# Adding the gated products to the merged sum by accumulating transfers in place of VectorE additions

## Chip, cores and metric

One Trainium2 chip, one of its cores. The time is the device time of one execution in microseconds, as the median of several executions; the profile is one more execution, recorded by the hardware profiler. Engines: PE is TensorE (PEld its weight loads), DVE is VectorE, ACT is ScalarE, POOL is GpSimd, SP is SyncE, which issues most of the loads.

## What is computed

One layer of a decoder trunk on 256 tokens of width 2048, all in float32. Three token mixers run side by side (a gated recurrence `a`, a windowed attention `b`, a short convolution `c`), each gives a vector of width 1024 per token, and the part that matters here joins them:

```python
y_a = (o_a * jax.nn.silu(a_g)) @ w_proj_hgrn[l]
y_b = (o_b * jax.nn.silu(b_g)) @ w_proj_attn[l]
y_c = (o_c * jax.nn.silu(c_g)) @ w_proj_conv[l]
merged = jax.nn.sigmoid(m_a) * y_a + jax.nn.sigmoid(m_b) * y_b + jax.nn.sigmoid(m_c) * y_c
y = merged @ w_out[l]
x = layer_norm(ALPHA * x + y, ln_g[l], ln_b[l])
```

The gates `m_a`, `m_b`, `m_c` are 2048 columns each of the input projection `x @ w_in`; `merged` and `y` are 256 x 2048.

## The kernel before

Every product of matrices is made from float32 data split into two parts, `hi` (a cast on ACT, line 114) and `lo` (the remainder, a subtraction on DVE, line 115); three matmuls (hi*hi, lo*hi, hi*lo) stand for one. The weights stream from HBM in loads of 1 MB issued by SP into three buffers `raw`. `gemm` (line 165) walks a weight matrix in granules of 1 MB, splits each half granule and issues its matmuls into two PSUM accumulators, one for each half of the 256 tokens (`t` = 0, 1). Between half granules it calls `pump`, which advances a background task by one step.

The merge is the loop over the three branches (lines 742 to 762). For each branch and each half of the 2048 gate columns, `pair_of_groups` (line 667) makes the gate logits of 1024 columns by a scheme with fewer block products, eight or seven of them in turn (matmuls in lines 679 to 681), and leaves them in two tiles `sg`; ACT takes the sigmoid (line 749). Then for each of the two groups of 512 columns (`d` from 0 to 3 in all) `gemm` makes the branch's projection, and DVE multiplies it by the gate. In branch `a` that product is written to `merged[d]`. In branches `b` and `c` it is written back to `sg` (line 757) and added to `merged[d]` by a second instruction (line 758). There are four tiles `merged[d]` of 128 x 2 x 512, each 512 KB, and two tiles `sg`.

In the last half of branch `c`, `turn(merged[d], d)` (line 647) is queued as a background task for every finished tile: it transposes the tile on PE in four groups of 128 x 128 per PSUM bank (`mT`, line 270), casts and subtracts it into the tiles `m` (hi and lo), and for every other pair of blocks makes the sums `msums`. The tasks of d = 0 and 1 run during the projection of d = 2, the task of d = 2 during the projection of d = 3, and the task of d = 3 during the first output product, `gemm(a["w_out"][2], ...)`, which is followed by `pair_of_groups` on `w_out2`, the last quarter and the layer norm. The output product reads `m` of d = 0 first and of d = 3 last (steps k = 12 to 15 of 16).

The order on each engine is not written out by hand: a scheduler places the instructions, with a cost model of its own, and each engine then runs its list in order. A transposition that waits therefore holds up every matmul behind it in PE's list. GpSimd has next to nothing to do between the attention and the layer norm.

Of the kernel before, what the change touches and what calls it, by code (L numbers as in the profile page):

```python
# [13 lines left out]
ALU = mybir.AluOpType  # L14
# [36 lines left out]
def hybrid_kernel(ctx, tc, a, out):  # L51
    nc = tc.nc
# [14 lines left out]
    def t8(shape, name, dt=F32):  # L67
        return w8.tile(shape, dt, tag="w8", name=name)
# [16 lines left out]
    def split_to(dst, src):  # L85

        nc.scalar.copy(out=dst[:, :, 0], in_=src)
        nc.vector.tensor_sub(out=dst[:, :, 1], in0=src, in1=f32(dst[:, :, 0]))
# [77 lines left out]
    def gemm(src, xs, n, major):  # L166


        acc = accumulators()
        per = HALF // n  # L170
        kt = src.shape[0] * 2 * per
        k = 0
        for g in range(src.shape[0]):
            raw = load_granule(src[g])
            for s in range(2):
                hi, lo = split_w(raw[:, s])
                for j in range(per):
                    xk = xs[k // 4][:, k % 4]
                    for b in range(2):
                        c = slice(b * P, b * P + P)  # L180
                        if major == "rows":
                            w = slice(j * n, j * n + n)
                            rows(acc[b][:, :n], xk, hi[:, w], lo[:, w], c, k == 0, k == kt - 1)
                        else:
                            w = slice(j * n + b * P, j * n + b * P + P)
                            columns(acc[b], xk, hi[:, w], lo[:, w], k == 0, k == kt - 1)
                    k += 1
                pump()
        return acc
# [395 lines left out]
    for hf in range(2):  # L585
# [11 lines left out]
        for u in range(2):  # L597
# [3 lines left out]
                             in1=C["gn"][:, hf * NC : hf * NC + NC].rearrange("p (o n) -> p o n", o=1)  # L601
# [51 lines left out]
    def turn(m, d):  # L653
        dst = t8([P, 4, 2, T], "m", F32R)
        ms.append(dst)
        if d % 2 == 0:
            msums.append(t8([P, 2, 4, 2, P], "msums", F32R))
        for i, ps in transpose_pairs([[m[:, t, c * P : c * P + P] for t in range(2)] for c in range(4)], "mT"):
            split_to(dst[:, i : i + 2], ps)
            if PAIRS[2 * d + i // 2]:  # L660
                raw = mgp.tile([P, 2, T], F32, tag="u", name="mraw")
                nc.scalar.copy(out=raw, in_=ps)
                sx = mgp.tile([P, 4, P], F32, tag="one", name="sx")
                block_sums([sx[:, j] for j in range(4)], raw[:, 0, :P], raw[:, 1, :P], raw[:, 0, P:], raw[:, 1, P:])
                split_to(msums[d // 2][:, d % 2], sx)
            yield
# [72 lines left out]
    merged = [mgp.tile([P, 2, NC], F32, tag="merged", name="merged", bufs=4) for _ in range(4)]  # L739
    mix = {"b": yb, "c": yc}  # L740
    for n, (wp, br) in enumerate((("w_proj_hgrn", "a"), ("w_proj_attn", "b"), ("w_proj_conv", "c"))):
        if n:
            for i in range(2):
                outs[br].append(t8([P, 4, 2, T], "o" + br, F32R))
                split_to(outs[br][i], mix[br][:, 4 * i : 4 * i + 4])
        for half in range(2):
            sg = pair_of_groups(a["w_gate"][2 * n + half], xs, sums, n > 0, 2 if n else 1)
            for y in sg:
                nc.scalar.activation(out=y, in_=y, func=AF.Sigmoid)
            if br == "c" and half:  # L750
                tasks.extend(turn(merged[d], d) for d in range(2))
            for j in range(2):
                d = 2 * half + j
                acc = gemm(a[wp][d], outs[br], NC, "rows")
                for t in range(2):
                    if n:
                        nc.vector.tensor_mul(out=sg[j][:, t], in0=acc[t], in1=sg[j][:, t])
                        nc.vector.tensor_add(out=merged[d][:, t], in0=merged[d][:, t], in1=sg[j][:, t])
                    else:
                        nc.vector.tensor_mul(out=merged[d][:, t], in0=acc[t], in1=sg[j][:, t])  # L760
                if br == "c" and half:
                    tasks.append(turn(merged[d], d))

# [167 lines left out]
```

## Time and profile before

| what | value |
|---|---|
| median of 3 runs | 1001.27 us (1000.53 to 1001.45) |
| the profiled execution | 999.9 us, of which the profile's span is 998.0 us |
| PE busy | 984.2 us (99% of the span) |
| DVE busy | 800.5 us (80%) |
| ACT busy | 561.0 us (56%) |
| POOL busy | 31.7 us (3%) |
| DMA | 193.67 MB, mean 194 GB/s over the span |

The table is to be read with the stages in mind. A share of busy time is a mean over the span, and an engine may be idle at one place because it waits there for another. The time of the profiled execution is 1.4 us below the median of the runs; sums are made against it. The span begins with the first instruction and leaves out 1.9 us around it.

### The profile page before, as it was taken

The page shows a single profiled execution, that of the slowest core. Times are in us where ns is not written, and L with a number is a line of the kernel's source. Part 1 is how long each engine was busy: PE and PEld are TensorE (multiplying, and loading weights), DVE is VectorE, ACT ScalarE, POOL GpSimd, SP SyncE. Part 2 cuts the span into 40 slices and gives each one's busy share as a digit, 9 for nine tenths or more (in the row PEclk, how much of TensorE's full clock was granted, in tenths as well). Part 3 has the DMA queues.
Part 4 walks back from the last instruction along what each step waited for, and adds up shares of the span by engine and source line. Part 5 has one row for each costly group of instructions (what it writes and reads, how often), then busy time and mean ns, then how long its engine had stood idle before and what let it go on. Part 6 is the DMA issues. An engine that isn't in the chain of part 4 may idle for free.

```text
span 998.0 us, 13720 instructions
## 1 busy us (share of the span) xinstructions
PE 984.2 (99%) x5430; PEld 828.8 (83%) x5430; DVE 800.5 (80%) x1001; ACT 561.0 (56%) x736; POOL 31.7 (3%) x32
## 2 busy tenths in 40 slices
PE   9999999999999999999999999999999999999995
PEld 6888888888888888888888888888888888888885
DVE  6556689969996666767778898887989889897997
ACT  6454568556576555645655555555555555564551
POOL 1000100020001000000000000000000000000003
PEclk9999999999999999999999999999999999999998
DMA  8755544344455446544555655565655555548542
GB/s 342 253 197 173 206 169 171 146 152 170 169 208 179 181 152 205 175 169 169 196 183 189 227 187 203 207 211 200 214 179 209 210 192 214 185 169 340 208 169 84
DMA packets 30687, 193.67 MB, mean 194 GB/s; under 512 B 3824, under 2 KB 4880, under 8 KB 8352
## 3 DMA queue, kind: packets, MB, share of 16 engines
q1 hardware_dynamic: 28800, 185.90, 52.1%
q10 hardware_dynamic: 1152, 4.72, 1.2%
q0 software_dynamic: 672, 2.20, 0.8%
q8 instruction: 42, 0.69, 0.3%
q14 instruction: 21, 0.17, 0.1%
HBM read 190.68 MB, written 2.12 MB: 193 GB/s over the span
## 4 chain that ended last, share of the span: by engine, by line
PE 92%; DVE 5%; issue 1%; ACT 1%; DMA 1%; POOL 0%; SPq 0%; DVEq 0%; ACTq 0%
PE acc L162 24%; PE acc L161 11%; PE p L679 9%; PE p L680 9%; PE p L681 9%; PE acc L154 8%; PE acc L156 8%; PE acc L155 8%; PE sc L472 1%; DVE lo L115 1%; PE acc L164 1%; PE bg L156 1%; PE bg L154 1%; PE bg L155 1%; PE pvb L514 1%
## 5 line engine op out<-in xcount | busy, mean ns | idle before, releaser
L114 ACT CAST hi<-raw 128x1024 fp32r<-128x1024 f32 (+1 forms) x341 | 343.2, 1013 | 317.4 <-PE p L680 105.0
L115 DVE TENSOR_TENSOR lo<-raw,hi 128x1024 fp32r<-128x1024 f32 (+1 forms) x341 | 398.6, 1179 | 109.4 <-ACT hi L114 107.8
L162 PE MATMUL acc<-xs,hi 128*128 128x512 f32 x1056 | 372.8, 397 | 0.0
L161 PE MATMUL acc<-xs,lo 128*128 128x256 f32 x990 | 279.4, 282 | 0.2 <-DVE lo L115 0.2
L162 PEld LDWEIGHTS acc<-xs,hi 128*128 128x128 f32 x1056 | 197.5, 188 | 44.3 <-issue 1.5
L161 PEld LDWEIGHTS acc<-xs,lo 128*128 128x128 f32 x990 | 186.9, 189 | 4.2 <-issue 1.2
L679 PE MATMUL p<-hi,xs 128*128 128x512 f32 x240 | 93.5, 389 | 0.0
L680 PE MATMUL p<-hi,xs 128*128 128x512 f32 x240 | 93.5, 389 | 0.0
L681 PE MATMUL p<-lo,xs 128*128 128x512 f32 x240 | 93.5, 389 | 0.0
L115 DVE TENSOR_TENSOR lw<-w,hw 128x2048 fp32r<-128x2048 f32 x28 | 64.2, 2293 | 22.2 <-ACT hw L114 20.8
L114 ACT CAST hw<-w 128x2048 fp32r<-128x2048 f32 x28 | 53.5, 1911 | 9.1 <-DVE w L706 8.9
L681 PEld LDWEIGHTS p<-lo,xs 128*128 128x128 f32 x240 | 45.1, 188 | 9.4
L680 PEld LDWEIGHTS p<-hi,xs 128*128 128x128 f32 x240 | 45.1, 188 | 9.3
L679 PEld LDWEIGHTS p<-hi,xs 128*128 128x128 f32 x240 | 45.1, 188 | 9.3
L154 PE MATMUL acc<-hi,xs 128*128 128x512 f32 (+1 forms) x128 | 47.6, 372 | 0.3 <-ACT hi L114 0.3
L199 ACT COPY rest<-acc 128x256 f32<-128x256 f32 x66 | 23.8, 372 | 41.3 <-PE acc L162 40.7
L155 PE MATMUL acc<-hi,xs 128*128 128x512 f32 (+1 forms) x128 | 46.6, 364 | 0.0
L156 PE MATMUL acc<-lo,xs 128*128 128x512 f32 (+1 forms) x128 | 46.1, 364 | 0.0
L704 DVE TENSOR_TENSOR w<-raw 128x1024 f32<-128x1024 f32 x28 | 34.1, 1219 | 0.7 <-DMA raw<-in_w_gate 0.2
L154 PEld LDWEIGHTS acc<-hi,xs 128*128 128x128 f32 x128 | 24.3, 190 | 6.5 <-ACT hi L114 2.2
L680 PE MATMUL p<-hw,sums 128*128 128x512 f32 x72 | 28.0, 390 | 0.0
L679 PE MATMUL p<-hw,sums 128*128 128x512 f32 x72 | 28.0, 389 | 0.0
(269 smaller groups left out, 1505.9 us busy)
## 6 DMA issues: line engine op xcount, KB each, us to landing
raw<-in_w_cols SPq DMA_DIRECT2D x68, 1024.0 KB, 4.8
raw<-in_w_gate SPq DMA_DIRECT2D x48, 1024.0 KB, 4.8
raw<-in_w_out SPq DMA_DIRECT2D x16, 1024.0 KB, 4.8
raw<-in_w_rows SPq DMA_DIRECT2D x8, 1024.0 KB, 4.7
raw<-in_w_proj_hgrn SPq DMA_DIRECT2D x8, 1024.0 KB, 4.8
raw<-in_w_proj_attn SPq DMA_DIRECT2D x8, 1024.0 KB, 4.8
raw<-in_w_proj_conv SPq DMA_DIRECT2D x8, 1024.0 KB, 4.8
raw<-in_w_first SPq DMA_DIRECT2D x6, 1024.0 KB, 7.2
```

The costliest lines, as they stand in the source:

```text
L114: nc.scalar.copy(out=hi, in_=r)
L115: nc.vector.tensor_sub(out=lo, in0=r, in1=f32(hi))
L154: nc.tensor.matmul(out=acc, lhsT=xk[:, 0, ts], rhs=hi, start=first, stop=False)
L155: nc.tensor.matmul(out=acc, lhsT=xk[:, 1, ts], rhs=hi, start=False, stop=False)
L156: nc.tensor.matmul(out=acc, lhsT=xk[:, 0, ts], rhs=lo, start=False, stop=last)
L161: nc.tensor.matmul(out=acc[:, :T], lhsT=lo, rhs=xk[:, 0], start=False, stop=False)
L162: nc.tensor.matmul(out=acc, lhsT=hi, rhs=xk, start=first, stop=last)
L199: nc.scalar.copy(out=rest[p], in_=acc[p, T:])
L679: nc.tensor.matmul(out=ps, lhsT=x[0], rhs=hi, start=begins, stop=False)
L680: nc.tensor.matmul(out=ps, lhsT=x[1], rhs=hi, start=False, stop=False)
L681: nc.tensor.matmul(out=ps, lhsT=x[0], rhs=lo, start=False, stop=last)
L704: nc.vector.tensor_sub(out=w[:, 0:2], in0=raw[:, 0:1].to_broadcast([P, 2, NC]), in1=raw[:, 1::2])
```

## The change

In branches `b` and `c` the 16 additions on DVE (128 x 512 each) are taken out. After both halves `t` of a group have been multiplied, one transfer issued by GpSimd adds the whole tile `sg` (128 x 1024) to `merged[d]` in SBUF, eight transfers of 512 KB in all.

```diff
@@ -755,9 +755,10 @@
                 for t in range(2):
                     if n:
                         nc.vector.tensor_mul(out=sg[j][:, t], in0=acc[t], in1=sg[j][:, t])
-                        nc.vector.tensor_add(out=merged[d][:, t], in0=merged[d][:, t], in1=sg[j][:, t])
                     else:
                         nc.vector.tensor_mul(out=merged[d][:, t], in0=acc[t], in1=sg[j][:, t])
+                if n:
+                    nc.gpsimd.dma_start(out=merged[d], in_=sg[j], accum_op=ALU.add)
                 if br == "c" and half:
                     tasks.append(turn(merged[d], d))
```

Lines below the merge move down by one. The scheduler moves instructions too. On PE the matmuls stand in the same order as before; what moves are the transpositions of d = 2 and d = 3. For d = 2 (during the last projection of branch `c`, whose operands are named `oc`), the difference, where a minus is before and a plus is the change:

```order
-L270 MATMUL mT<-ident,merged 128x128
-L154 MATMUL acc<-hi,oc 128x512
-L155 MATMUL acc<-hi,oc 128x512
-L156 MATMUL acc<-lo,oc 128x512
-L270 MATMUL mT<-ident,merged 128x128 x3
...
+L154 MATMUL acc<-hi,oc 128x512
+L270 MATMUL mT<-ident,merged 128x128 x4
 L155 MATMUL acc<-hi,oc 128x512
 L156 MATMUL acc<-lo,oc 128x512
```

The first transposition of d = 2 stood 12 matmuls behind the last group of transpositions of d = 1; now 22 matmuls stand between them, and its second group of four follows two matmuls behind the first.

For d = 3 (during the first output product, whose operands are named `m`), again on PE:

```order
 L156 MATMUL acc<-lo,m 128x512
-L270 MATMUL mT<-ident,merged 128x128 x4
 L154 MATMUL acc<-hi,m 128x512
...
 L155 MATMUL acc<-hi,m 128x512
+L270 MATMUL mT<-ident,merged 128x128 x4
 L156 MATMUL acc<-lo,m 128x512
 L270 MATMUL mT<-ident,merged 128x128 x4
```

The first group of transpositions of d = 3 stood behind 12 matmuls of the output product; now it stands behind 23, and one matmul ahead of the second group.

On DVE, around the last two groups of branch `c` (d = 2 ahead, d = 3 behind):

```order
 L757 TENSOR_TENSOR sg<-acc,sg 128x512 x2
 L88 TENSOR_TENSOR m<-mT,m 128x2x256
-L758 TENSOR_TENSOR merged<-merged,sg 128x512 x2
+L115 TENSOR_TENSOR lo<-raw,hi 128x1024
...
+L757 TENSOR_TENSOR sg<-acc,sg 128x512
 L555 TENSOR_TENSOR sx<-mraw,sx 128x128
+L757 TENSOR_TENSOR sg<-acc,sg 128x512
...
-L757 TENSOR_TENSOR sg<-acc,sg 128x512 x2
-L758 TENSOR_TENSOR merged<-merged,sg 128x512 x2
```

The additions are gone, a subtraction `lo` of the weights comes one place earlier in their stead, and the products of d = 3 come ahead of a `lo` and the sums `msums` that stood ahead of them. On POOL the eight transfers stand behind the attention's loads of the bias and ahead of the layer norm, with nothing between them.

## Rows read from the trace of the kernel before

**Rows 1.** The page: busy time, share of the span and instructions of each engine.

```profile
PE 984.2 (99%) x5430; PEld 828.8 (83%) x5430; DVE 800.5 (80%) x1001; ACT 561.0 (56%) x736; POOL 31.7 (3%) x32
```

**Rows 2.** Waits of PE, whole span: who waited, total us, times, longest us.

```profile
PE warm L582 <- DVE lneps L219: 1.5, 1, 1.5
PE acc L156 <- DVE l L115: 0.6, 1, 0.6
```

**Rows 3.** The tile merged: ns min/median/max of one, first and last start in us.

```profile
L270 PEld LDWEIGHTS mT<-ident,merged x32: 137/140/143, 877.5 to 905.9; 128*128 128x128 f32 x32
L758 DVE TENSOR_TENSOR merged<-merged,sg x16: 680/683/687, 699.0 to 901.6; 128x512 f32<-128x512 f32 x16
```

**Rows 4.** Timeline of DVE around d = 2 and d = 3: start us, duration us.

```profile
887.90 1.28 DVE L757 TENSOR_TENSOR sg<-acc,sg 128x512 f32<-128x512 f32 x2
889.69 1.29 DVE L758 TENSOR_TENSOR merged<-merged,sg 128x512 f32<-128x512 f32 x2
...
899.79 1.28 DVE L757 TENSOR_TENSOR sg<-acc,sg 128x512 f32<-128x512 f32 x2
900.99 1.28 DVE L758 TENSOR_TENSOR merged<-merged,sg 128x512 f32<-128x512 f32 x2
...
924.32 2.29 DVE L115 TENSOR_TENSOR lw<-w,hw 128x2048 fp32r<-128x2048 f32 x1 [0.25 <-ACT hw L114]
```

**Rows 5.** Timeline of PE, same columns: start, middle, transpositions, end.

```profile
1.46 3.79 PE L582 MATMUL warm<-warm 128*128 128x512 f32 x4 [1.46 <-DVE lneps L219]
...
877.75 0.60 PE L270 MATMUL mT<-ident,merged 128*128 128x128 f32 x4
...
890.58 0.27 PE L270 MATMUL mT<-ident,merged 128*128 128x128 f32 x1
...
899.48 0.39 PE L156 MATMUL acc<-lo,oc 128*128 128x512 f32 x1
899.71 0.39 PE L154 MATMUL acc<-hi,m 128*128 128x512 f32 x1
...
902.43 0.60 PE L270 MATMUL mT<-ident,merged 128*128 128x128 f32 x4
...
928.36 0.39 PE L681 MATMUL p<-lw,msums 128*128 128x512 f32 x1
...
986.47 0.28 PE L156 MATMUL acc<-lo,m 128*128 128x256 f32 x1
```

**Rows 6.** DMA issues: tiles, issuing queue, count, KB each, median us from issue to landing.

```profile
raw<-in_w_out SPq DMA_DIRECT2D x16, 1024.0 KB, 4.8
...
bias<-bias_dr POOLq DMA_DIRECT2D x2, 1024.0 KB, 7.1
...
lbt<-in_ln_b ACTq DMA_DIRECT2D x1, 1024.0 KB, 12.5
...
oh<-in_onehot POOLq DMA_DIRECT2D x1, 48.0 KB, 2.1
```

**Rows 7.** Windows: stretch, busy us by engine, PEclk, DMA share, GB/s.

```profile
890.00:898.00 8.00, 8.00 (x41) 6.50 (x40) 7.90 (x16) 5.82 (x8) 0.00 (x0) 1.00 0.36 131
898.00:906.00 8.00, 8.00 (x42) 6.61 (x40) 4.97 (x8) 1.23 (x3) 0.00 (x0) 1.00 0.95 380
906.00:914.00 8.00, 8.00 (x38) 6.60 (x36) 6.85 (x11) 6.44 (x8) 0.00 (x0) 1.00 0.97 383
...
989.00:990.00 1.00, 0.00 (x0) 0.00 (x0) 1.00 (x3) 0.74 (x2) 0.58 (x1) 0.55 0.00 0
```

**Rows 8.** Timeline of ACT's queue: the four loads for the layer norm.

```profile
898.11 0.87 ACTq L768 DMA_DIRECT2D xres<-in_x  x2
...
899.55 0.50 ACTq L771 DMA_DIRECT2D lbt<-in_ln_b  x1
```

**Rows 9.** Timelines of POOL and DVE at the first load of the bias.

```profile
314.88 0.96 POOL L453 DMA_DIRECT2D bias<-bias_dr  x1
...
314.94 2.16 DVE L438 SCALAR_TENSOR_TENSOR oa<-pv,rs,ga 128x128 f32<-128x128 f32 x8 [1.79 <-POOL rs L433]
```

## Prediction

> **What bounds the kernel now.** Read the page's busy times first: PE works 99% of the span, DVE 80%, POOL 3% [rows 1]. Then the waits of PE, to see whether some other engine still paces it anywhere: the list is four entries long, and behind the 1.5 us of the start its longest is 0.6 us, one matmul of the last output quarter that waits for a `lo` of DVE [rows 2]. So the matmul stream sets the time. Work taken from DVE can give back those 0.6 us at most, and a new wait inside PE's list costs its full length. The reader should therefore look for the places where PE has to wait for the merged sum. The timelines show two: the transpositions of d = 2 and of d = 3, which stand in PE's list shortly after the tile is finished. Before, the addition of d = 3 ends at 902.27 and the transposition starts at 902.43 [rows 4, 5].
>
> **What goes.** 16 additions of 0.683 us, 10.9 us of DVE time [rows 3]. All but the last four lie beside matmuls that never wait for them; the four of d = 2 and 3 lie between product and transposition. Worth in the sum: 0, as PE does not wait for DVE there; at most the 0.6 us of [rows 2].
>
> **What comes, and costs nothing.** Eight issues on POOL, which is idle from the attention to the layer norm; a comparable issue lasts 0.96 us [rows 9]. The first six transfers (branch `b`, and d = 0 and 1 of `c`) are read again only tens of microseconds later; the next writer of a tile `sg` comes a whole pair of gate groups later, too. These six are covered by that distance; without it each would cost a landing. 4 MB join the 193.67 MB that the DMA engines move, and PE waits for no load now. The reordering on DVE puts the subtraction `lw` of the first summed pair of `w_out2` behind two residual updates and four statistics. It ended at 926.61 for a matmul at 928.36, 1.75 us of room [rows 4, 5]; the second update and the statistics put some 2.7 us ahead of it, of which 1.1 us return because one `lo` is done earlier. So 0 to 0.7 us; I take 0, since PE arrives later at that place by the stalls below.
>
> **What comes, and costs.** The two last tiles. The question at each is how long after the product the accumulated tile lands, against how long PE has other work.
>
> *Room at d = 2.* The products end at 887.90 + 1.28 = 889.18 [rows 4]. PE's list now has 22 matmuls between the transpositions of d = 1 and those of d = 2. Twelve of them are through at 890.58, ten more take 0.23 us each, so PE arrives at 892.9; its weight load, which is the one that reads the tile, begins 0.25 us earlier (877.5 against 877.75) [rows 3, 5]. Room: 892.65 - 889.2 = 3.45 us.
>
> *Room at d = 3.* The last projection matmul ends at 899.48 + 0.39 = 899.87, and the second product is now ahead of `lo` and `msums`, so it ends some 0.7 us later, at 900.6 [rows 4, 5]. The output product starts at 899.71; 12 matmuls later, at 902.43, the transpositions stood before, which is 0.227 us for one; 23 matmuls later PE is at 904.9, its weight load at 904.65 [rows 5]. Room: 4.05 us.
>
> *Price of one landing.* No accumulating transfer is in the trace, so bounds. A small load from POOL's queue lands after 2.1 us, one of 1 MB in runs of 1 KB after 7.1; a load of 1 MB in long rows from SP's queue after 4.8 [rows 6]. Beyond the fixed 2.1 us that is 2.7 to 5.0 us for a MB, on average 3.8. A plain copy of 512 KB at the quicker rate would land after 3.45 us. An addition has to read both tiles: 1 MB read for 512 KB written. At the mean rate that is 2.1 + 3.8 = 5.9 us, at the slower 7.1. I take 5.9, between them, because the rows of `sg` (4 KB) lie between the two loads' runs. The Trainium skill, "Collectives: The Full Stack", section "The bandwidth ceiling", says of the same adder that it costs nothing itself but needs two source reads, and so halves the rate; no run here shows it. By that rule alone the doubling would stand, and a plain-rate landing would drop out.
>
> *d = 2*: 5.9 - 3.45 = **2.45 us** of PE standing still. Ends: 0 (plain copy) and 3.65 (slower rate).
>
> *d = 3*: the DMA engines are busy to 0.36 of their time while d = 2 would travel, but to 0.95 and 0.97 from 898 to 914 [rows 7], as ACT issues four loads of 1 MB from 898.11 on, the last of which needs 12.5 us [rows 6, 8]. If the transfer shares the engines half and half, its moving part doubles: 2.1 + 7.6 = 9.7 us; undisturbed it is 5.9. I take the middle, 7.8, because the loads before it are already part done at 900.6. 7.8 - 4.05 = **3.75 us**. Ends: 0 and, behind all four loads (899.55 + 12.5 = 912.05), 11.45 - 4.05 = 7.4 us.
>
> After each stall PE finds its operands ready, but it makes nothing up, as it was never short of them. The later chain of d = 3 has room: step k = 12 of the output product comes 49 matmuls (11 us) behind the transpositions.
>
> *PE's clock.* The last matmul ends at 986.75, and in the stretch from 989 to 990 the granted clock averages 0.55, so it fell from 2.4 to 1.2 GHz after at least 2.3 us of rest [rows 5, 7]. A rest of 3.75 us could do the same. The price is bounded by the start, where PE works from 1.46 on and the pace settles only behind the warm-up matmuls, which take 3.79 us [rows 5]: at half pace for some 4.7 us, 2.4 us lost. I take 0, as one end of work is no proof for a short gap, and keep 2.4 for the upper end.
>
> **Sum.** 2.45 + 3.75 = 6.2 us on the profiled execution's 999.9, so 1006.1; that execution is 1.4 us under the median of 1001.27, and against the median the same 6.2 give **1007.5 us**.
>
> **Rivals.**
> - *Landing at the rate of a plain copy* (17%), which ends not slower. The mechanism is the room itself: PE waits only where a landing exceeds 3.45 and 4.05 us. For it: 3.45 us by SP's loads. Against it: the second read. At d = 2 no wait, at d = 3 with half the engines 2.1 + 2.7 - 4.05 = 0.75 us: 1002.0, no change that a measurement can tell (about 0.2%, 2 us).
> - *The transfer of d = 3 waits behind ACT's loads* (18%). For it: a DMA share of 0.95 to 0.97 over 16 us. Against it: loads from several queues are in flight together before as well. 3.65 + 7.4 us and the clock's 2.4: 13.5 us, 1014.8.
> - *GpSimd cannot write its transfer's descriptors while DVE works* (4%). DVE has some 4.3 us of work behind the products of d = 2 (`m`, two `lo`, sums) and 1.7 behind those of d = 3 before it waits for PE itself, so the two landings would be later by that: 6.2 + 6.0, 1013.5. Against it: the bias load was issued in 0.96 us beside DVE's 2.16 us of products [rows 9]. The Trainium skill, "SBUF — State Buffer", section "Who interferes with whom", has such a lock for copies in DVE's two-port modes, and says that `tensor_tensor` contends only with GpSimd's reads; by that rule this rival falls, and the row agrees.
> - *DVE was pacing PE after all* (3%): the 0.6 us wait and more go, with landings inside the room. Against it: [rows 2]. Faster by more than 2 us needs waits that are not in the list.
>
> **Chances and range.** The forecast has the remaining 58%. Faster by over 0.2%: 0.03, the last rival. Within 0.2%: 0.17, the first. Slower: 0.80, all others. The range goes from the first rival's 1002.0 to just past the second's, 1016; outside it I leave a quicker result and a landing that is slower than every row here.
>
> **What would show it.** Two new entries in PE's waits, both of transpositions `mT` and both ended by a transfer, 2 to 3 us at d = 2 and 3 to 5 at d = 3, and no other; DVE with 16 instructions fewer and some 11 us less; transfers `merged<-sg` that land after 5 to 8 us, the last slowest; the span longer by the sum of the two waits. Wrong if PE waits for neither (then the landings are under 4 us), if it waits at any earlier `merged` or `sg`, or if matmuls after the stall run at half pace.

## The result: slower by 1.4%

The changed kernel takes 1016.1 us as the median of four runs (1014.27 to 1016.18), the kernel before, beside it, 1001.05 us (1000.53 to 1001.45). The ratio is 1.0144, with a 95% interval from 1.0129 to 1.0159. The profiled execution of the changed kernel took 1016.03 us with a span of 1014.1; that of before took 999.9 with a span of 998.0. The spans differ by 16.1 us, and this is the sum that the trace has to explain.

The busy times on the page of the changed kernel (for before, see [rows 1]):

```profile
PE 987.9 (97%) x5430; PEld 831.3 (82%) x5430; DVE 793.6 (78%) x985; ACT 559.5 (55%) x736; POOL 38.8 (4%) x40
```

DVE has 16 instructions less, as foretold, but only 6.9 us of busy time less and not 10.9; the other groups of its instructions kept their durations, so presumably the records of the additions had overlapped their neighbours'; this is not shown. POOL has 8 issues and 7.1 us more. PE executes the same 5430 instructions and still is busy 3.7 us longer: some of them ran slower. Its waits over the whole span (who waited, total us, times, longest us) answer to [rows 2]:

```profile
PE mT L270 <- DMA merged<-sg: 12.2, 2, 10.1
PE warm L582 <- DVE lneps L219: 1.5, 1, 1.5
PE acc L156 <- DVE l L115: 0.6, 1, 0.6
```

The list has one new entry, two waits of the transpositions for a transfer. The wait of 0.6 us for DVE, which was the most that DVE's relief could have given back, is still there. The transfers of the tile `merged` (durations of the issues min/median/max in ns, first and last start in us; [rows 3] before), and under them the time from a transfer's issue to its landing:

```profile
L761 POOL DMA_DIRECT2D merged<-sg x8: 852/862/955, 699.7 to 905.4; - x8
...
DMA to landing us min/median/max: 5.2/6.0/13.4
```

The critical chain from 886 to 925 us tells which landing is which (start us, duration us): d = 2 needs 5.30 us, d = 3 needs 13.39.

```profile
889.72 5.30 DMA merged<-sg
...
905.43 13.39 DMA merged<-sg
```

What the DMA queues moved in that time (packets, MB, share of the 16 engines; by the loads' sizes and issuers q0 is POOL's queue, q1 SP's, q10 ACT's), first from 891.1 to 894.7 us at d = 2, then from 905.4 to 909.7 and from 909.7 to 918 at d = 3:

```profile
q0 software_dynamic: 144, 0.52, 94.3%
q1 hardware_dynamic: 23, 0.19, 12.5%
...
q10 hardware_dynamic: 172, 1.29, 95.8%
...
q10 hardware_dynamic: 169, 1.25, 38.8%
q1 hardware_dynamic: 132, 1.05, 31.7%
q0 software_dynamic: 133, 0.52, 31.6%
```

At d = 2 the transfer's 0.52 MB start 1.4 us after the issue and are through 3.6 us later. At d = 3 not a byte of it moves for 4.3 us after the issue; only ACT's loads do. Then its 0.52 MB need up to 918, some 8 us, beside 2.3 MB of two other queues. So the landing has grown in two parts, a late start and a slow passage.

PE's timeline at the two places (start, duration, in brackets the idle time before it; [rows 5] before):

```profile
892.62 0.39 PE L154 MATMUL acc<-hi,oc 128*128 128x512 f32 x1
...
895.15 1.09 PE L270 MATMUL mT<-ident,merged 128*128 128x128 f32 x4 [2.14 <-DMA merged<-sg]
...
908.51 0.39 PE L155 MATMUL acc<-hi,m 128*128 128x512 f32 x1
...
918.96 1.09 PE L270 MATMUL mT<-ident,merged 128*128 128x128 f32 x4 [10.06 <-DMA merged<-sg]
```

Four transpositions took 0.60 us before and take 1.09 behind each wait. The windows (stretch, busy us by engine, PEclk, DMA share, GB/s; [rows 7] before) show why:

```profile
895.00:898.00 3.00, 2.85 (x11) 2.58 (x12) 0.86 (x2) 1.55 (x3) 0.00 (x0) 0.50 0.58 246
899.00:908.00 9.00, 9.00 (x41) 7.48 (x40) 5.62 (x11) 3.21 (x4) 0.86 (x1) 1.00 0.60 202
912.00:919.00 7.00, 0.04 (x1) 0.07 (x2) 0.00 (x0) 0.00 (x0) 0.00 (x0) 0.51 1.03 359
919.00:922.00 3.00, 3.00 (x12) 2.62 (x13) 0.71 (x2) 1.23 (x3) 0.00 (x0) 0.50 0.96 404
```

The granted clock is 0.50 in the 3 us behind the first rest, back at 1.00 from 899 to 908, and again 0.50 in the 3 us behind the second rest: the fall from 2.4 to 1.2 GHz. During the second rest the DMA engines are busy all the time. ACT's queue and POOL at that place (start us, duration us; [rows 8] before):

```profile
904.57 0.86 ACTq L769 DMA_DIRECT2D xres<-in_x  x2
905.47 0.45 ACTq L771 DMA_DIRECT2D lg<-in_ln_g  x1
905.95 0.63 ACTq L772 DMA_DIRECT2D lbt<-in_ln_b  x1
```

```profile
905.43 0.86 POOL L761 DMA_DIRECT2D merged<-sg  x1 [14.85 <-DVE sg L757]
```

Before, ACT issued these loads 2.5 us ahead of the end of d = 3's product (898.11 against 900.59, as worked out ahead). Now the first of them goes out only 0.9 us ahead of the transfer, so none is part done when the transfer comes. SP's next load, of the weights, follows at 906.29, 0.9 us behind the transfer.

**The account.** At d = 2 the last matmul has given way at 892.62 + 0.23 = 892.85, and the transposition starts at 895.15: 2.3 us. At d = 3 it is 908.51 + 0.23 = 908.74 to 918.96: 10.2 us. The matmuls behind each rest run at half pace for some 3.4 us, up to about 898.5 and 922.4, and lose half of that: 2 x 1.7. Together 15.9 of the 16.1 us.

### The profile page after: what moved, and what is told of

Read it like the earlier page. It is cut to its first block, busy times and chain, and to the rows that moved or that the text cites. A ratio compares the mean times of both kernels' runs of the same rounds, so it can differ in the third digit from the quotient of the medians.

```text
span 1014.1 us, 13736 instructions
## 1 busy us (share of the span) xinstructions
PE 987.9 (97%) x5430; PEld 831.3 (82%) x5430; DVE 793.6 (78%) x985; ACT 559.5 (55%) x736; POOL 38.8 (4%) x40
## 3 DMA queue, kind: packets, MB, share of 16 engines
q0 software_dynamic: 1824, 6.39, 3.4%
q10 hardware_dynamic: 1152, 4.72, 1.3%
HBM read 190.68 MB, written 2.12 MB: 190 GB/s over the span
## 4 chain that ended last, share of the span: by engine, by line
PE 87%; issue 6%; DVE 4%; DMA 2%; ACT 0%; POOL 0%; SPq 0%; ACTq 0%; DVEq 0%; POOLq 0%
PE acc L162 23%; PE acc L161 11%; PE p L680 8%; PE p L679 8%; PE p L681 8%; PE acc L154 7%; PE acc L156 7%; PE acc L155 7%; DMA merged<-sg 2%; PE sc L472 1%; PE acc L164 1%; PE bg L155 1%; PE bg L154 1%; PE bg L156 1%; PE pvb L514 1%
## 5 line engine op out<-in xcount | busy, mean ns | idle before, releaser
L115 DVE TENSOR_TENSOR lw<-w,hw 128x2048 fp32r<-128x2048 f32 x28 | 64.2, 2292 | 16.1 <-ACT hw L114 14.7
```

The lines of the kernel that those rows point to most:

```text
L115: nc.vector.tensor_sub(out=lo, in0=r, in1=f32(hi))
```

## Experiments

The question that the trace leaves open is the 13.39 us of d = 3: does it come from all that is in flight there, wherever it was issued, or from what was issued ahead of the transfer? Beside it stand the six transfers that were costed at nothing, the relief of DVE, and the clock. All kernels below are edits of the changed kernel; "ratio" is against the kernel before on the same chip. Those without a ratio were run once, with a profile.

### Additions of d = 2 and 3 on DVE again

```diff
-                if n:
+                if n and not (br == "c" and half):
                     nc.gpsimd.dma_start(out=merged[d], in_=sg[j], accum_op=ALU.add)
+                elif n:
+                    for t in range(2):
+                        nc.vector.tensor_add(out=merged[d][:, t], in0=merged[d][:, t], in1=sg[j][:, t])
```

> The last two groups of branch c (d = 2 and 3) are added by VectorE again, the other six by transfers. Theory (the whole loss lies in the two waits for the merged sum of d = 2 and 3 and in the slow matmuls behind them; the six other transfers are covered): no transposition waits for a transfer, time 1001 us, within 1 us of the kernel before. Rival (the eight transfers also cost by their traffic or their issue, wherever they are): the six keep three quarters of such a cost, so 1004 us or more. Second rival (the VectorE time that was freed is worth something once the waits are gone): 999 us or less.

Measured: 1000.53 us (1000.04 to 1002.1), ratio 0.9999 [0.9989, 1.0008]. The landings of the six transfers:

```profile
DMA to landing us min/median/max: 5.2/6.0/7.0
```

PE waits for no transfer here; its longest wait behind the start is again 0.6 us. The six transfers with distance behind them cost nothing, and the twelve additions that DVE no longer makes give nothing. The whole loss lies at d = 2 and 3.

### Addition of d = 3 alone on DVE

The same edit with `br == "c" and d == 3`.

> Only d = 3 is added by VectorE, d = 2 still by a transfer. Theory: the wait of d = 2 stays (2.1 to 2.3 us) and so do the slow matmuls behind it (1.7 us, granted clock 0.50 there), that of d = 3 goes (10.1 us and 1.7 us): 1005 us. Rival (the clock fell only because both stalls came close together, and a single short rest leaves it alone): 1003.3 us and a granted clock of 1.00 throughout.

Measured: 1003.84 us, span 1002.0. PE's waits, and its timeline at d = 2:

```profile
PE mT L270 <- DMA merged<-sg: 2.1, 1, 2.1
...
PE p L681 <- DVE lw L115: 0.9, 1, 0.9
```

```profile
895.20 0.63 PE L270 MATMUL mT<-ident,merged 128*128 128x128 f32 x4 [2.12 <-DMA merged<-sg]
```

The same 2.1 us as in the changed kernel, but the four transpositions behind it take 0.63 us and not 1.09: here the clock did not fall. So d = 2's wait is one thing and the fall behind it another, which comes in some executions and not in others. The time is near the rival's 1003.3 us, but the rival's reason, that both stalls came close together, doesn't explain it: the fall behind d = 2 comes before the second stall, and in two profiles below with both stalls (scale and shift later, work for PE) the clock stayed up at d = 2 as well. The wait of 0.9 us for `lw` is new. It is the subtraction that was costed at nothing because PE would arrive late there; without the stall of d = 3 PE arrives earlier, and waits.

### The loads behind the transpositions

ACT's four loads are issued when d = 3's transpositions are in PE's list, and not ahead of them.

```diff
+            if d == 3 and i == 2:
+                xr.extend(t8([P, D], f"xres{t}") for t in range(2))
+                for t in range(2):
+                    nc.scalar.dma_start(out=xr[t], in_=a["x"][t * P : t * P + P])
...
-    for t in range(2):
-        nc.scalar.dma_start(out=xr[t], in_=a["x"][t * P : t * P + P])
```

(`lg` and `lb` move with them.)

> All eight additions by transfers as in the change, but the four loads of 1 MB for the layer norm are issued behind the transpositions of d = 3 and not 0.9 us before its transfer. Theory (the transfer of d = 3 lands after 13.4 us and not 5.3 because it shares the DMA engines with these four loads): it lands after 5 to 6.5 us, PE waits 2 to 3 us there and not 10, time 1008 to 1009 us. Rival (this transfer is slow by itself, behind the weights' loads or whatever else is in flight there): it still lands after 11 us or more, time 1014 us or more.

Measured: 1008.71 us (1007.58 to 1009.98), ratio 1.0076 [1.0061, 1.0091]; d = 3 lands after 6.42 us. PE's waits:

```profile
PE mT L270 <- DMA merged<-sg: 5.3, 2, 3.1
```

The landing is halved and the wait falls from 10.1 to 3.1 us. ACT's loads are the cause of the difference. This doesn't say yet whether by their bytes or by their place.

### A plain copy in place of the accumulation

`accum_op=ALU.add` is left out, so the kernel leaves out the sum: each transfer overwrites `merged`.

> The eight transfers copy sg to merged and add nothing, so the sum is left out (only the last branch's product remains). Theory (the second read is what makes a transfer land late): the first six land after 3.5 to 4.2 us and not 5.2 to 6.0, d = 2 waits under 0.7 us, d = 3 still waits 6 us or more beside the four loads, time 1009 to 1012 us. Rival (issue and the fixed cost are what it costs, the addition is free): landings as in the change, 5.2 us or more, time 1015 us or more.

Measured: 1011.61 us. PE's waits and the tile `merged`:

```profile
PE mT L270 <- DMA merged<-sg: 8.4, 1, 8.4
```

```profile
L761 POOL DMA_DIRECT2D merged<-sg x8: 528/528/562, 700.7 to 902.5; - x8
...
DMA to landing us min/median/max: 2.9/3.1/11.8
```

A plain copy lands after 2.9 us at the least and 3.1 in the median, an accumulating transfer of the same 512 KB after 5.2 and 6.0 (7.0 at the most where ACT's loads are not beside it). So accumulating costs some 2.3 to 2.9 us, and without it d = 2 does not wait. That the second read is what costs this is the prediction's reason; the run doesn't tell the read from the addition. But beside the loads even the plain copy needs 11.8 us. What the accumulation itself adds, 1.6 us, is the smaller part of d = 3.

### Scale and shift later, the two loads of x ahead as before

The loads of `lg` and `lb` move behind the second summed pair of `w_out2`.

> As the change, but two of ACT's four loads (the layer norm's scale and shift) are issued some 35 us later; the two loads of the residual stay just ahead of the transfer of d = 3. Theory (the landing is late by the traffic it shares the engines with, in proportion): it lands after 8.5 to 10.5 us, between 6.4 and 13.4, PE waits 5 to 7 us there, time 1011 to 1013 us. Rival (it stands behind the loads that were issued ahead of it, the two of the residual, and the two behind it do not matter): it still lands after 12 us or more, time 1015 us or more.

Measured: 1018.66 us. PE's waits:

```profile
PE mT L270 <- DMA merged<-sg: 11.1, 2, 9.0
PE acc L156 <- DVE l L115: 3.4, 1, 3.4
```

The landing of d = 3 falls only from 13.39 to 12.31 us, though half of the loads' bytes are gone. By the theory of traffic, in proportion, it should have come to 8.5 to 10.5. This speaks for the place: of the four loads two are issued ahead of the transfer (902.75 against 903.60 here) and two behind it, and the two behind hardly matter. The kernel is slower on the whole because the postponed loads bring a wait of 3.4 us for DVE elsewhere; that wait is 0.6 in the changed kernel. Behind it the granted clock is 0.50 from 983 to 989 us.

### More room before the transpositions

```diff
-    def turn(m, d):
+    def turn(m, d, later=0):
+        for _ in range(later):
+            yield
...
-                    tasks.append(turn(merged[d], d))
+                    tasks.append(turn(merged[d], d, 2 if d == 2 else 3))
```

> As the change, with all loads where they were, but the transpositions stand later in PE's list: those of d = 2 behind 36 matmuls and not 22, those of d = 3 behind 48 and not 23. Theory (a landing costs only what it exceeds the room by): no wait at d = 2; at d = 3 the room is 9.7 us against 13.4, so a wait of 3 to 4 us, time 1004 to 1006.5 us. Rival (the late landing moves the whole later chain, so that the output product runs out of operands behind the transpositions): the wait at d = 3 shrinks, but new waits on the tile m appear, and the time stays above 1009 us.

Measured: 1999.73 us. PE was busy for 1983.6 us with the same 5430 matmuls that took 987.9 in the changed kernel, far from the merge too, so this says nothing on the edit.

### Room, and the loads behind

The edit before with 2 for both tiles, together with the loads behind the transpositions.

> All eight additions by transfers; the transpositions of d = 2 and d = 3 both stand 36 matmuls late, and the four loads are issued behind those of d = 3. Theory (with landings of 5.3 and 6.5 us the room of 6.5 and 7 us covers both): PE waits for no transfer, time 1000.5 to 1001.5 us, no different from the kernel before. Rival (VectorE's 10.9 us of freed time are worth something once nothing waits): 999 us or less.

Measured: 1000.34 us (999.5 to 1000.91), ratio 0.9997 [0.9988, 1.0006], the lowest of all kernels and not to be told from before. PE's waits:

```profile
PE warm L582 <- DVE lneps L219: 1.5, 1, 1.5
PE acc L156 <- DVE l L115: 0.6, 1, 0.6
...
```

All 16 additions are off DVE, no transfer is waited for, and the time is that of before: the relief of DVE is worth nothing here. No run of the idea was faster.

### Work for PE during the rest

In `turn`, ahead of d = 3's transpositions, 40 matmuls whose result is never read.

```diff
+        if d == 3:
+            yield
+            idle = bank("idle")
+            for _ in range(40):
+                nc.tensor.matmul(out=idle, lhsT=C["ones"], rhs=ms[0][:, 0], start=True, stop=True)
```

> As the change, but ahead of the transpositions of d = 3 PE's list has 40 further matmuls (9.1 us) whose result nobody reads, in the time in which PE otherwise rests. Theory (the slow matmuls behind the wait come from the clock that fell while PE rested): the granted clock stays at 1.00 there, the matmuls behind the transpositions start every 0.23 us at once, time 1014.4 us, 1.7 us under the change. Rival (they are slow because they follow a wait for a transfer, whatever the clock): pace of 0.57 us as in the change and a time of 1016 us or more.

Measured: 1014.83 us (1012.17 to 1016.34), ratio 1.014 [1.0126, 1.0154]; the profiled run is the one of 1012.17. The times overlap those of the changed kernel (1014.27 to 1016.18), so the answer is in the trace. Its timeline of PE:

```profile
906.95 9.50 PE L662 MATMUL idle<-m,ones 128*128 128x512 f32 x40
916.90 0.63 PE L270 MATMUL mT<-ident,merged 128*128 128x128 f32 x4 [0.46 <-DMA merged<-sg]
```

The landing is unchanged (13.36 us), but behind it four transpositions take 0.63 us and not 1.09, so the slow matmuls go with PE's rest and the clock and not with the late transfer. In this run the clock stayed up at d = 2 too, where nothing had been filled in; but in every other profile with a rest of 3.1 us or more at d = 3, slow matmuls followed it.

### Room once more

> The kernel of e6_room once more, as that run was at half pace from end to end and told nothing. The transpositions of d = 2 stand 36 matmuls later and those of d = 3 48 matmuls later; all four loads of ACT stay where they were. Theory (room): the landing of d = 3 keeps its 12 to 13.5 us, as nothing that it meets has changed, and only what exceeds the room is left as a wait. The first deferral adds 36 x 0.227 = 8.2 us of room at d = 2, so none is left there; the second adds 10.9 us against a wait of 10.2 (less 0 to 2, since the product of d = 3 comes earlier against PE), so 0 to 1.5 us at d = 3: 999.5 to 1003. Rival (the loads must be moved as well): the wait only moves along, because without d = 2's wait the loads start later against the transfer and it lands after 15 us or more: a wait of 3 us or over, 1003.5 to 1007.

Measured: 1003.76 us, span 1002.0. PE's waits, and the issues of POOL and ACT at d = 3:

```profile
PE acc L154 <- ACT hi L114: 1.6, 1, 1.6
```

```profile
900.24 0.86 POOL L763 DMA_DIRECT2D merged<-sg  x1 [9.86 <-DVE sg L759]
```

```profile
903.69 1.02 ACTq L771 DMA_DIRECT2D xres<-in_x  x2
```

PE waits for no transfer. Both expectations missed, though the time lies in the rival's range: nothing that the rival named happened. The landing of d = 3 is 5.6 us, neither 12 to 13.5 nor 15: with the transpositions of d = 2 deferred and no rest there, the last product is done early, and the transfer goes out 3.45 us ahead of the loads. What moves the product against ACT's loads thus decides the landing as well; with the loads 3.45 us behind the transfer, more room alone is enough to take both waits away. The time lies over the expected 999.5 to 1003 because of a new wait that isn't a transfer's: ACT's casts of the tiles `m` of d = 3 stand ahead of the casts `hi` of the next weights in ACT's order, and so these wait for the late transpositions too (1.6 us).

### The same loads, just behind the transfer

This tells bytes from place. POOL copies one column into each of the two `xres` tiles behind the transfer's issue, so that ACT can issue its loads only after that.

```diff
+        nc.gpsimd.tensor_copy(out=xr[t][:, 0:1], in_=sg[1][:, 1, 0:1])
         nc.scalar.dma_start(out=xr[t], in_=a["x"][t * P : t * P + P])
```

> ACT's four loads are issued just behind the transfer of d = 3 instead of 0.9 us ahead of it: a copy of one column by POOL, behind the transfer's issue, writes into the tiles that the first two loads fill, so that ACT issues them about 1 us after the transfer. The traffic is the same 4 MB at almost the same time; only the order is turned. Theory A (the transfer stands behind what was issued ahead of it): the landing of d = 3 falls to 6 to 7.5 us, the wait to 3 to 4 us, and the time to 1007 to 1010, as in e3_loads_in_turn. Theory B (the engines are shared by all that is in flight): the landing stays at 10 to 13 us, the wait at 7 to 10 and the time at 1012 to 1016.

Measured: 1008.44 us (1007.42 to 1010.07), ratio 1.0074 [1.0054, 1.0094]. The critical chain, PE's waits, ACT's queue, and what the DMA queues moved from 906.6 to 911.2 us:

```profile
905.24 6.57 DMA merged<-sg
```

```profile
PE mT L270 <- DMA merged<-sg: 5.3, 2, 3.2
```

```profile
906.74 1.81 ACTq L770 DMA_DIRECT2D xres<-in_x  x2
...
909.30 0.66 ACTq L773 DMA_DIRECT2D lbt<-in_ln_b  x1
```

```profile
q0 software_dynamic: 142, 0.52, 80.9%
q1 hardware_dynamic: 53, 0.43, 22.9%
```

The same four loads go out from 1.5 us behind the transfer on, all of them while it is still in flight (up to 911.81), and it lands after 6.57 us, as if they weren't there (6.42 without them). Moving the loads by 2.4 us against the transfer takes 6.8 us off the landing. The queues show why: all the transfer's bytes are through before ACT's queue (q10) moves any. SP's load, issued at 906.11, has moved 0.43 MB by then; it may be why the landing is 6.57 and not the 5.3 of d = 2. Theory A held: what decides is whether ACT's loads were issued ahead.

### One load ahead

The third experiment with the first load of `x` left at its place.

> One load of ACT (the first half of x) stays ahead of the transfer of d = 3; the other three are issued behind the transpositions of d = 3. None ahead gave a landing of 6.4 us, two ahead 12.3, four ahead 13.4. Theory A (it stands behind what was issued ahead): half of the way, 8.5 to 10 us, a wait of 5 to 6.7 us, 1009 to 1013. Rival (it is one transfer among queues that take turns, however much stands in each): any load beside it costs the same as two, 11.5 to 12.5 us, a wait of 8 to 9 us, 1012.5 to 1015. Second rival (only a pile of loads matters): 6.4 to 7 us, 1007 to 1009.

Measured: 1013.5 us. The critical chain, PE's waits, the DMA issues from 902.7 to 907 us (median us from issue to landing), and what the queues moved from 905.8 to 909.2 and from 909.2 to 914.9 us:

```profile
905.85 9.64 DMA merged<-sg
```

```profile
PE mT L270 <- DMA merged<-sg: 8.4, 2, 6.3
```

```profile
raw<-in_w_out SPq DMA_DIRECT2D x1, 1024.0 KB, 9.3
merged<-sg POOLq DMA_DIRECT2D x1, 512.0 KB, 9.6
```

```profile
q10 hardware_dynamic: 121, 0.99, 94.2%
...
q1 hardware_dynamic: 132, 1.02, 47.2%
q0 software_dynamic: 136, 0.52, 46.6%
```

The landing lies within theory A's 8.5 to 10, the time 0.5 us over its range: the clock fell at both places here. The dose runs 6.4 to 6.6 us with none ahead, 9.6 with one, 12.3 with two, 13.4 with two ahead and two at once behind: about 3 us for each of the first two MB ahead. The queues show that the MB ahead doesn't simply add its own time. Until 909.2, 3.4 us after the issue, only ACT's load moves; then the transfer needs up to 914.9, 5.7 us, because SP's load, issued 0.9 us *behind* it, moves 1.02 MB at the same time. So a load ahead delays the start, and a transfer that has not started shares the engines with what was issued behind it as well. SP's load needs 9.3 us too, so POOL's transfer isn't treated worse than a load from another queue.

### Halves

Each half is added by a transfer of its own, right behind its product.

```diff
                         nc.vector.tensor_mul(out=sg[j][:, t], in0=acc[t], in1=sg[j][:, t])
+                        nc.gpsimd.dma_start(out=merged[d][:, t], in_=sg[j][:, t], accum_op=ALU.add)
...
-                if n:
-                    nc.gpsimd.dma_start(out=merged[d], in_=sg[j], accum_op=ALU.add)
```

> Each half (T = 512 columns, 256 KB) is added by a transfer of its own right behind its product, so 16 transfers instead of 8. Theory (the part of a landing that moves bytes is what counts): undisturbed, half the bytes land after 2.1 + (5.3 - 2.1) / 2 = 3.7 us, so the wait at d = 2 falls from 2.1 us to 0.5 to 1; at d = 3 the first half is issued at about the time of ACT's loads and the second behind them, with 6.5 to 11 us to landing and a wait of 3 to 8: 1006 to 1012. Rival (the descriptors and the fixed part count): two issues of 0.5 to 0.9 us each on POOL put the second half no earlier than the whole, the waits stay at 2 and 9 to 10: 1014 to 1016.

Measured: 1018.14 us. PE's waits, the landings, POOL's DMA queue on the page, and what SP's queue moved from 889.3 to 897.1 us:

```profile
PE mT L270 <- DMA merged<-sg: 12.6, 4, 6.0
```

```profile
DMA to landing us min/median/max: 3.3/7.7/11.7
```

```profile
q0 software_dynamic: 2976, 6.39, 3.1%
...
q1 hardware_dynamic: 144, 1.05, 40.0%
```

In the changed kernel the queue has 1824 packets for the same 6.39 MB; the 1152 more are 144 for each of eight more transfers. One half alone lands after 3.3 us, but the pair is not quicker than the whole: at d = 2 the second half is waited for until 897.1, where the whole had landed at 895.0. SP's load, issued at 890.60, 1.3 us behind the second half, moved all of its 1.05 MB in that time, against 0.19 MB while the whole transfer's bytes moved in the changed kernel. Halving the bytes did not halve the price, as the rival said; the expected times of both were under the measured one.

## Why the prediction was wrong in size and right in kind

- **The bound** held. PE was at 99% and nothing else paced it: a kernel with all additions off DVE and no wait for a transfer takes 1000.34 us, the time of before. Neither 10.9 us of additions nor the 0.6 us of [rows 2] came back. The third rival fell as well: at d = 2 POOL issued in 0.86 us from 889.72 on, while DVE was at a `lo` from 889.70 to 890.92.
- **The places** held. PE waits at d = 2 and d = 3 and nowhere else, and the six other transfers cost nothing. The subtraction `lw` that was costed at nothing is not in PE's list either. That it comes from the stalls, as the prediction has it, fits the run without d = 3's stall, where PE waited 0.9 us for it; the runs with no stall at all show no such wait.
- **d = 2** held nearly. Forecast: landing 5.9, wait 2.45. Measured: 5.30 and 2.3 (2.14 in the profile's count of idle time). Part of this is luck. The sum counted the landing from the end of the products, but the products ended at 889.19 and POOL's issue started at 889.72, 0.5 us later, a delay that was costed at nothing; the landing was 0.6 us shorter than forecast, and the two nearly cancel. That accumulating lengthens the landing shows in the plain copy's 2.9 to 3.1 us; that its second read does it is the prediction's reason and was not tested by itself. The Trainium skill's rule in "Collectives: The Full Stack", section "The bandwidth ceiling", that two source reads halve the rate, agrees with this pair in kind: 5.2 to 6.0 us (least and median) against 2.9 to 3.1, not quite double.
- **d = 3 is the step that failed**: "If the transfer shares the engines half and half, its moving part doubles ... undisturbed it is 5.9. I take the middle, 7.8, because the loads before it are already part done at 900.6." It landed after 13.39 us, which makes a wait of 10.2 us and not 3.75. Three things were wrong in it. The transfer didn't start beside the loads: for 4.3 us only ACT's loads moved, where the sum had the transfer moving among them from the start. Then its bytes took some 8 us and not the 3.6 of d = 2, beside two other queues. This part alone is near the doubling of the sentence (7.6 us), but the middle between shared and undisturbed halved the increase. And the loads were not part done: their issue was taken from [rows 8], from a kernel without the rest at d = 2. ACT issues them with its cast of `msums`, which waits for DVE's sums; the rest at d = 2 and DVE's new order moved both, so that the loads went out at 904.57, 0.9 us ahead of the transfer. Even the end that was kept for the range, 7.4 us "behind all four loads", counted from the old issue at 899.55. The room shrank too: 908.74 - 0.25 - 905.43 = 3.1 us and not 4.05, as product and issue came later against PE.
- **The clock** was taken as 0 with 2.4 us as the end. It fell behind both rests and cost some 1.7 us each, 3.4 of the 16.1. This term was put at nothing although [rows 7] had shown a fall after 2.3 us of rest at the end of the program and the forecast rest of d = 3 was longer. Matmuls at half pace behind a stall were one of the prediction's own signs of being wrong, and it came.
- **The sum**: forecast 6.2 us over the profiled time of before, measured 16.1. 2.45 became 2.3, 3.75 became 10.2, 0 became 3.4. The measured 1016.1 us lies 0.1 us past the upper end of the range, near where the second rival stood: "the transfer of d = 3 waits behind ACT's loads", 13.5 us and 1014.8. That rival named what started the delay; it had been given 18%. It had the wait behind all four loads, and the transfer landed at 918.8, before the last two of them (920.2 and 922.7). What was set against it, that loads from several queues are in flight together, is true as well: it is the second part of the landing.

The Trainium skill's "DMA: Bandwidth & Descriptors", section "Queues, rings and completion order", says that a DMA engine takes turns between the queues that have work, a packet at a time. The trace agrees for the second part of d = 3's landing: from 909.7 to 918 us three queues move side by side, 0.52, 1.25 and 1.05 MB. It shows no such turns in the first part, where for 4.3 us ACT's queue alone moves 1.29 MB, nor in the run with the loads just behind, where POOL's 0.52 MB are through before ACT's queue moves anything. How much a queue may move before another has its turn, these runs don't show.

What stays open is why the clock falls behind a rest of 2.1 us in some executions (1.09 us for four transpositions behind it in the changed kernel) and not in others (0.63 with d = 3's addition on DVE): the rests were alike. In four profiles with a fall at d = 2 they were 2.11 to 2.16 us, in three without one 2.12.

## What to carry to other kernels

Before work is moved from an idle engine's slack to a transfer, look for what has to read the result next: with tens of microseconds between, the transfer is free; with three or four, what its landing exceeds them by is on the path. Price the landing in two parts: the start, which loads issued ahead on another queue delay, and the passage, which whatever has been issued by then slows. Take the moment of those issues from the kernel as it will be, stalls included, not from the trace of before. In this kernel the order against bulk loads was worth more than the size: loads issued 2.4 us later gave 6.8 us on the landing, and smaller pieces gave nothing.

## What the runs showed of the hardware that was not expected

- Where none of ACT's loads were beside it, an accumulating transfer of 512 KB from SBUF to SBUF landed 5.2 to 7.0 us after its issue (median 6.0), a plain copy after 2.9 at the least and 3.1 in the median; its issue occupied POOL for 0.86 us against 0.53.
- With one, two loads of 1 MB issued 0.9 us ahead on another engine's queue it landed after 9.6, 12.3 us; with four issued from 1.5 us behind it on, after 6.57. Behind one load its bytes started 3.4 us after the issue and not 1.4, and then took 5.7 us beside a load that had been issued 0.9 us behind it.
- Two halves of 256 KB cost the queue twice the packets (144 for each transfer, of 512 KB or of 256 KB) and landed no earlier than the whole.
- Behind a rest of PE of 2.1 us the granted clock was 0.50 in four profiles, the changed kernel's among them, and 1.00 in three; each of the two falls in the changed kernel cost some 1.7 us.
